# Grouped-query attention on one core: a repeating table of steps, with three of sixteen score tiles on VectorE

## The chip, the cores and the metric

The kernel runs on one core of one Trainium2 chip. The metric is device time in microseconds (us). Three timed runs of the kernel before took 431.78, 433.16 and 433.04 us; the median is 433.04 us. A profile of one execution goes with them.

## The reference

Q has 8 batches, 512 queries, 32 heads and 64 columns; K and V have 8 K heads, and four Q heads share each K head.

```python
K_expanded = np.repeat(K, heads_per_group, axis=2)
V_expanded = np.repeat(V, heads_per_group, axis=2)
...
scores = np.einsum('bhqd,bhkd->bhqk', Q, K_expanded) * scale
weights = np.exp(scores - np.max(scores, axis=-1, keepdims=True))
weights = weights / (np.sum(weights, axis=-1, keepdims=True) + 1e-10)

output = np.einsum('bhqk,bhkd->bhqd', weights, V_expanded)
```

All arrays are float32. `scale` is 1/8.

## The kernel before

The kernel takes exp of the scaled scores without subtracting a maximum, sums the rows with an extra column of ones beside V, and checks afterwards that the sums lie within bounds. If they do not, a second, slow path (`general_path`) runs; with these inputs it does not. Both kernels have it, and it plays no part here.

**Units, jobs, pairs, tiles.** A unit is two K heads of one batch, so there are 32 units. A job is one K head with its four Q heads, so a unit holds two jobs and the kernel 64. A job has two pairs of Q heads. Scores are held transposed: 128 keys on the partitions, 512 queries along them. One tile is the scores of one pair against 128 keys, that is two heads of 512 queries, 1024 columns. A pair has four such tiles, a job 8, a unit 16.

**The way of a tile.** TensorE writes it into PSUM with two matmuls of 64 contraction rows (`scores`, L209). Of the 8 tiles of a job, seven go through `s_ps` (two buffers) to ScalarE, whose exp (L227) writes float16 weights into `pt`. The eighth goes through `d_ps` (one buffer, shared with the transposes) to VectorE, which makes exp out of bits in a chain of five instructions:

- u (L238): scale and add, from PSUM to int16 in SBUF
- f (L259, in `exp_d2`): the low ten bits of u
- g (L251) and w (L255): a quadratic correction; in most jobs (`by_pool`) both run on GpSimd, in the first three and in the last on VectorE
- the join (L272, in `exp_d4`): u + w, written into `pt` as the bits of a float16

g, w and the join read and write SBUF alone, as f does. u reads PSUM.

**Weights times V.** For each pair, 32 matmuls of 65 columns (L303, `pv`) accumulate in `pv` (one buffer). VectorE then takes the reciprocal of the sums (L336) and multiplies (L340, `norm`), reading PSUM, into `o_sb`, which SyncE stores (L380).

**Transposes and loads.** Q comes in through GpSimd's DMA queue with a cast to bfloat16, a transfer for each unit (L126). TensorE transposes it (L164), VectorE copies it out of PSUM (L167). K is loaded for each batch (L103) and transposed by SyncE's DMA queue. V is loaded for each batch in four transfers (L111). `check_v` (L177, L184) multiplies each V head with itself to bound its size.

**Order.** The schedule is manual: each engine works through its own instructions in the order in which the program issues them, which is the loop over jobs at L423 to L505. In it, the parts of job j (scores and exp) alternate with those of job j-1 (`pv` and `norm`). Around VectorE's chain it reads:

```python
        if late and by_pool(last):
            exp_d4(last)
        exp_d2(j)
```

So the join of the last job comes directly ahead of f of this job, and GpSimd's g and w start only after f.

Of the kernel before, what the change touches and what calls it, by code (L numbers as in the profile page):

```python
# [36 lines left out]
WIDE = lambda j: False  # L37
# [21 lines left out]
def fast_path(ctx, tc, Q, K, V, out, flag):  # L59
# [7 lines left out]
    NPAIR = HPG // 2  # L67
    scale = 1.0 / math.sqrt(D)
    A_U = 1024.0 / math.log(2.0) * scale
    B_U = 15.0 * 1024.0 + 1024.0 * math.log2(EXP_S)  # L70
    SPB = 16

    const_pool = ctx.enter_context(tc.tile_pool(name="const", bufs=1))
    qnat_pool = ctx.enter_context(tc.tile_pool(name="qnat", bufs=4))
# [4 lines left out]
    dve_pool = ctx.enter_context(tc.tile_pool(name="dve", bufs=2))  # L79
    osb_pool = ctx.enter_context(tc.tile_pool(name="osb", bufs=3))  # L80
    inv_pool = ctx.enter_context(tc.tile_pool(name="inv", bufs=3))
# [14 lines left out]
    vt = [const_pool.tile([128, SC, KV, D + 1], BF16, name=f"v{j}") for j in range(2)]  # L96
# [11 lines left out]

    def load_v(b, lo=0, hi=KV):
        for sc in range(SC):  # L110
            nc.gpsimd.dma_start(  # L111
                out=vt[b % 2][:, sc, lo:hi, 0:D],
                in_=V[b, sc * 128:(sc + 1) * 128, lo:hi, :],
            )

    def load_v_head(b, g):
        nc.gpsimd.dma_start(
            out=vt[b % 2][:, :, g, 0:D], in_=V[b, :, g, :].rearrange("(sc p) d -> p sc d", p=128)
        )

    def load_q(u, cuts=(0, 2 * HPG)):
        b, gp = divmod(u, GP)
        h0 = gp * 2 * HPG
        qn[u] = qnat_pool.tile([128, SC, 2 * HPG, D], BF16, name="q_nat")
        for lo, hi in zip(cuts[:-1], cuts[1:]):
            nc.gpsimd.dma_start(  # L126
                out=qn[u][:, :, lo:hi, :],
                in_=Q[b, :, h0 + lo:h0 + hi, :].rearrange("(sc p) h d -> p sc h d", p=128),
            )
# [3 lines left out]

# [21 lines left out]

    def trans_q(j, bank, lo=0, hi=NPAIR):
        u, g = divmod(j, 2)
        ps = bank.bitcast(BF16).rearrange("p (i sc c) -> p i sc c", i=NPAIR, sc=SC)  # L160
        for i in range(lo, hi):
            for sc in range(SC):
                h = g * HPG + 2 * i
                nc.tensor.transpose(ps[:, i, sc, :], qn[u][:, sc, h:h + 2, :], ident)  # L164
        if u not in qt:
            qt[u] = qt_pool.tile([128, 2, NPAIR, S], BF16, name="qt")
        return lambda: nc.vector.tensor_copy(  # L167
            out=qt[u][:, g, lo:hi, :], in_=ps[:, lo:hi, :, :].rearrange("p i sc c -> p i (sc c)")
        )


    def check_v(u, bank):
        b, gp = divmod(u, GP)
        for g in range(2):
            for sc in range(SC):
                v = vt[b % 2][:, sc, 2 * gp + g, 0:D]
                nc.tensor.matmul(  # L177
                    bank[64 * g:64 * g + 64, 0:D],
                    v,
                    v,  # L180
                    start=(sc == 0),
                    stop=(sc == SC - 1),
                )
        return lambda: nc.vector.tensor_reduce(  # L184
            out=okv[:, u:u + 1], in_=bank[:, 0:D], op=ALU.max, axis=AX.X
        )

    NJOB = NU * 2  # L190
    DPAIR = NPAIR - 1

    def taken(j):
        return 3 if WIDE(j) else 2

    def act_tiles(j):
        every = [(i, kc, m) for i in range(NPAIR) for kc in range(SC) for m in range(2)]
        first = DPAIR * SC * 2
        mine = [n for n in range(len(every)) if not first <= n < first + taken(j)]
        groups = [[n for n in mine if n // 2 == h] for h in range(len(every) // 2)]  # L200
        return [[every[n] for n in group] for group in groups if group]

    jobs, osb, invs, ends = {}, {}, {}, []

    def scores(j, ps, i, kc, m):
        u, g = divmod(j, 2)
        b, gp = divmod(u, GP)
        keys = kt_first[:, gp, :, :] if b == 0 else kt[b][:, :, gp, :]
        nc.tensor.matmul(  # L209
            ps,  # L210
            keys[64 * m:64 * m + 64, g ^ m, kc * 128:(kc + 1) * 128],
            qt[u][64 * m:64 * m + 64, g, i, :],
            start=True,
            stop=True,
        )

    def open_job(j):
        pt = pt_pool.tile([128, NPAIR, SC, 2, S], FP16, name="pt")
        jobs.setdefault(j, {}).update(pt=pt, pv={})

    def act_tile(j, n):
        group = act_tiles(j)[n]
        i, kc, lo = group[0]
        ps = s_pool.tile([128, 2, S], FP32, name="s_ps")
        for _, _, m in group:
            scores(j, ps[:, m, :], i, kc, m)
        nc.scalar.activation(  # L227
            out=jobs[j]["pt"][:, i, kc, lo:, :], in_=ps[:, lo:, :], func=EXP, scale=scale
        )

    def exp_d(j, lo, hi, ps):
        st = jobs.setdefault(j, {})
        if "u" not in st:
            for name, dtype in (("u", I16), ("f", I16), ("g", BF16), ("w", BF16)):
                st[name] = dve_pool.tile([128, 3, S], dtype, name=name + "16")[:, 0:taken(j), :]
        for n in range(lo, hi):
            scores(j, ps[:, n - lo, :], DPAIR, n // 2, n % 2)
        return lambda: nc.vector.tensor_scalar(  # L238
            out=st["u"][:, lo:hi, :], in0=ps[:, 0:hi - lo, :], scalar1=A_U, scalar2=B_U,
            op0=ALU.mult, op1=ALU.add,  # L240
        )


    def by_pool(j):
        return 3 <= j < NJOB - 1

    def correction(engine, f, g, w):
        as_bits = engine is nc.gpsimd  # L250
        engine.tensor_scalar(  # L251
            out=g, in0=f, scalar1=-EXP_F1, scalar2=EXP_K * 2.0 ** (24 * as_bits),
            op0=ALU.add, op1=ALU.mult,
        )
        engine.tensor_tensor(out=w, in0=g, in1=f.bitcast(FP16) if as_bits else f, op=ALU.mult)  # L255

    def exp_d2(j):
        st = jobs[j]
# [3 lines left out]
        if by_pool(j):  # L262
            exp_d3(j, nc.gpsimd)

    def exp_d3(j, engine):
        st = jobs[j]
        correction(engine, st["f"], st["g"], st["w"])

    def exp_d4(j):
        st = jobs[j]  # L270
        n = taken(j)
        nc.vector.tensor_tensor(  # L272
            out=st["pt"][:, DPAIR, :, :, :].rearrange("p kc m q -> p (kc m) q")[:, 0:n, :].bitcast(
                U16
            ),
            in0=st["u"],
            in1=st["w"],
            op=ALU.add,
        )

    def blocks(j, i):
        if j == NJOB - 1:
            kcs = (0, 1, 2, 3) if i == 0 else (2, 0, 1, 3)
        else:
            kcs = (2, 3, 1, 0)
        return [(kc, m, qc) for kc in kcs for m in range(2) for qc in range(SC)]

    def pv(j, i, lo, hi):
        st = jobs[j]
        u, g = divmod(j, 2)  # L290
        b, gp = divmod(u, GP)
        if lo == 0:

            if j < NJOB - 1:
                t = pv_pool.tile([128, 2, S], FP32, name="pv")
            else:
                t = d_tile() if i == 0 else s_pool.tile([128, 2, S], FP32, name="s_ps")
            t = t.rearrange("p m (qc c) -> p m qc c", qc=SC)
            st["pv"][i] = t[:, :, :, 0:D + 1]
        order = blocks(j, i)  # L300
        for n in range(lo, hi):
            kc, m, qc = order[n]
            nc.tensor.matmul(  # L303
                st["pv"][i][:, m, qc, :],
                st["pt"][:, i, kc, m, qc * 128:(qc + 1) * 128],
                vt[b % 2][:, kc, 2 * gp + g, :],
                start=(n < 2 * SC and qc == 0),
                stop=(n >= len(order) - 2 * SC and qc == SC - 1),
            )
# [11 lines left out]
    def norm(j, i):  # L321
        st = jobs[j]
        u, g = divmod(j, 2)
        sums = st["pv"][i]
        if u not in osb:
            osb[u] = osb_pool.tile([128, SC, 2 * HPG, D], FP32, name="o_sb")
        p = j * NPAIR + i
        left = NJOB * NPAIR - p
        k, n = divmod(p, SPB)
        if left <= NLAST:  # L330
            inv = inv_last[:, NLAST - left]
        else:
            if k not in invs:
                invs[k] = inv_pool.tile([128, SPB, 2, SC], FP32, name="inv")
            inv = invs[k][:, n]
        nc.vector.reciprocal(out=inv, in_=sums[:, :, :, D:D + 1])  # L336
        if left == 1:
            last_check()
        h = g * HPG + 2 * i
        nc.vector.tensor_tensor(  # L340
            out=osb[u][:, :, h:h + 2, :].rearrange("p qc m d -> p m qc d"),
            in0=sums[:, :, :, 0:D],
            in1=inv[:, :, :, None].to_broadcast((128, 2, SC, D)),
# [4 lines left out]
        elif g == 1 and i == NPAIR - 1:  # L348
            store(u, 0, 2 * HPG)
        if left > NLAST and (n == SPB - 1 or left == NLAST + 1):  # L350
            cols = (n + 1) * 2 * SC
            flat = invs.pop(k).rearrange("p s m qc -> p (s m qc)")[:, 0:cols]
# [10 lines left out]

    def last_check():
# [8 lines left out]
        count = pv_pool.tile([128, 2, S], FP32, name="pv")  # L373
# [11 lines left out]

    def probe():
# [4 lines left out]
        correction(nc.gpsimd, f, g, w)  # L391
# [4 lines left out]


# [5 lines left out]
    for j in range(2):  # L403
        nc.gpsimd.memset(vt[j][:, :, :, D:D + 1], 1.0)
    load_v_head(0, 0)
# [218 lines left out]
```

## Time and profile before

| What | Value |
|---|---|
| median of the three runs | 433.04 us (431.78 to 433.16) |
| span of the profiled execution, first to last instruction | 431.5 us |
| what lies around the span, by the three times | 0.3 to 1.7 us |
| ScalarE busy | 413.5 us (96%) |
| TensorE busy | 392.3 us (91%) |
| VectorE busy | 309.3 us (72%) |
| GpSimd busy | 254.1 us (59%) |
| exp on ScalarE (L227) | 448 instructions, 412.2 us |
| steady part, 86.0 to 137.3 us | 51.3 us for four units |

The profile gives no total time for the profiled execution itself; its span is set against the three times. Busy time is the time in which at least one instruction of the engine was in work; neighbouring instructions overlap, so a mean duration times a count can be above it. TensorE's ends are modelled, so its 91% does not say that it is full. Shares over the whole span mix a start, a steady part and an end; here the steady part is long, from about 34 to 424 us.

### The profile page before, as it was taken

How to read it: one execution, taken by the hardware profiler on the slowest of the kernel's cores; microseconds unless marked ns; L12 is line 12 of the kernel's file. 1: busy time of each engine (PE TensorE's matmuls, PEld its weight loads, DVE VectorE, ACT ScalarE, POOL GpSimd, SP SyncE). 2: the span in 40 equal slices, each digit the busy share in tenths (PEclk: the TensorE clock that was granted, in tenths of full speed). 3: DMA queues.
4: the chain of work that ended last, by engine and by line, in shares of the span. 5: the costliest groups of instructions: out<-in, count | busy, mean ns of one | idle time of the engine just before them, and what ended most of it. 6: DMA issues, size and time to landing. Idle time of an engine off the chain costs nothing.

```text
span 431.5 us, 13531 instructions
## 1 busy us (share of the span) xinstructions
PE 392.3 (91%) x5945; PEld 249.6 (58%) x5945; DVE 309.3 (72%) x585; ACT 413.5 (96%) x449; POOL 254.1 (59%) x212
## 2 busy tenths in 40 slices
PE   6889999999999999999999999999999999999984
PEld 2455566556556556556556556566555655655653
DVE  2587778767777767776767876876777776777765
ACT  3889999999999999999999999999999999999993
POOL 8805464965468566595457756497546856545530
PEclk8599999999999999999999999999999999999998
DMA  9998645898649986499946979689954998622214
GB/s 101 173 167 186 171 137 146 124 182 202 154 128 195 143 201 150 119 212 125 259 78 161 191 89 287 149 115 196 204 143 136 187 156 195 151 99 99 99 72 130
DMA packets 91439, 66.97 MB, mean 155 GB/s; under 512 B 52080, under 2 KB 74608, under 8 KB 91376
## 3 DMA queue, kind: packets, MB, share of 16 engines
q0 software_dynamic: 56544, 25.17, 49.9%
q1 hardware_dynamic: 34832, 40.90, 34.9%
q8 instruction: 47, 0.77, 0.7%
q14 instruction: 16, 0.13, 0.1%
HBM read 50.33 MB, written 33.55 MB: 194 GB/s over the span
## 4 chain that ended last, share of the span: by engine, by line
ACT 65%; PE 28%; DVE 4%; issue 1%; POOL 1%; ACTq 0%; DVEq 0%; POOLq 0%
ACT pt L227 65%; PE s_ps L209 12%; PE pv L303 10%; PE d_ps L164 5%; DVE o_sb L340 1%; DVE w L255 0%; DVE pt L272 0%; POOL q_nat L126 0%; DVE qt L167 0%; DVE kt_first L146 0%; PE d_ps L143 0%; DVE g L251 0%; PE d_ps L145 0%; POOL k_nat L103 0%; ACTq L227 0%
## 5 line engine op out<-in xcount | busy, mean ns | idle before, releaser
L227 ACT ACTIVATE pt<-s_ps 128x1024 f16<-128x1024 f32 x448 | 412.2, 1115 | 9.6 <-PE s_ps L209 9.3
L303 PEld LDWEIGHTS <-pt 128*128 128x128 f16 x4096 | 142.8, 98 | 78.2 <-issue 56.1
L303 PE MATMUL pv<-v,pt 128*128 128x65 bf16 x4032 | 178.8, 195 | 3.5 <-DVE o_sb L340 2.5
L209 PE MATMUL s_ps<-qt,kt 64*128 64x512 bf16 x784 | 153.7, 382 | 23.8 <-ACT pt L227 8.6
L251 POOL TENSOR_SCALAR g<-f 128x1024 bf16<-128x1024 int16 x60 | 62.4, 1039 | 154.5 <-DVE f L259 154.5
L255 POOL TENSOR_TENSOR w<-g,f 128x1024 bf16<-128x1024 bf16 x60 | 127.5, 2125 | 5.0
L209 PEld LDWEIGHTS <-kt 64*128 64x128 bf16 x896 | 59.5, 93 | 62.6 <-issue 26.8
L340 DVE TENSOR_TENSOR o_sb<-pv,inv 128x512 f32<-128x512 f32 x125 | 86.4, 691 | 4.3
L336 DVE RECIPROCAL inv<-pv 128x8 f32<-128x8 f32 x125 | 25.7, 206 | 85.4 <-PE pv L303 85.4
L238 DVE TENSOR_SCALAR u<-d_ps 128x1024 int16<-128x1024 f32 x64 | 77.7, 1214 | 0.7 <-PE d_ps L209 0.7
L167 DVE COPY qt<-d_ps 128x1024 bf16<-128x1024 bf16 (+1 forms) x65 | 44.3, 683 | 20.1 <-PE d_ps L177 12.1
L272 DVE TENSOR_TENSOR pt<-u,w 128x1024 uint16<-128x1024 int16 x64 | 43.6, 681 | 0.2
L164 PE MATMUL d_ps<-ident,q_nat 128*128 128x128 bf16 x512 | 40.7, 224 | 0.9 <-DVE kt_first L146 0.9
L164 PEld LDWEIGHTS <-q_nat 128*128 128x128 bf16 x512 | 29.5, 99 | 16.0 <-issue 14.9
L259 DVE TENSOR_SCALAR f<-u 128x1024 int16<-128x1024 int16 x64 | 29.6, 463 | 0.1
L126 POOL DMA_DIRECT2D q_nat<-in_Q_dram x34 | 27.3, 803 | 1.5 <-DMA q_nat<-in_Q_dram 1.2
L111 POOL DMA_DIRECT2D v<-in_V_dram x32 | 28.2, 890 | 0.0
L209 PE MATMUL s_ps<-qt,kt_first 64*128 64x512 bf16 x112 | 24.4, 431 | 2.6 <-ACT pt L227 1.1
L209 PE MATMUL d_ps<-qt,kt 64*128 64x512 bf16 x112 | 21.4, 376 | 0.0
L209 PEld LDWEIGHTS <-kt_first 64*128 64x128 bf16 x128 | 7.6, 96 | 10.8 <-issue 6.5
L177 PE MATMUL d_ps<-v 128*64 128x64 bf16 x256 | 10.4, 201 | 0.0
L177 PEld LDWEIGHTS <-v 128*64 128x64 bf16 x256 | 6.9, 110 | 3.3 <-issue 0.2
(46 smaller groups left out, 52.4 us busy)
## 6 DMA issues: line engine op xcount, KB each, us to landing
out_dram<-o_sb SPq DMA_DIRECT2D x31, 1024.0 KB, 5.9
q_nat<-in_Q_dram POOLq DMA_DIRECT2D x31, 512.0 KB, 7.5
k_nat<-in_K_dram POOLq DMA_DIRECT2D x7, 512.0 KB, 7.7
v<-in_V_dram POOLq DMA_DIRECT2D x28, 128.0 KB, 8.8
kt<-kt SPq DMA_DIRECT2D x14, 256.0 KB, 4.2
out_dram<-o_sb SPq DMA_DIRECT2D x4, 256.0 KB, 2.4
kt<-k_nat SPq DMA_TRANSPOSE x28, 8.7
v<-in_V_dram POOLq DMA_DIRECT2D x4, 96.0 KB, 8.2
```

Source lines behind the costliest of these rows:

```text
L111: nc.gpsimd.dma_start(out=vt[b % 2][:, sc, lo:hi, 0:D], in_=V[b, sc * 128:(sc + 1) * 128, lo:hi, :],)
L164: nc.tensor.transpose(ps[:, i, sc, :], qn[u][:, sc, h:h + 2, :], ident)
L167: return lambda: nc.vector.tensor_copy(out=qt[u][:, g, lo:hi, :], in_=ps[:, lo:hi, :, :].rearrange("p i sc c -> p i (sc c)"))
L209: nc.tensor.matmul(ps, keys[64 * m:64 * m + 64, g ^ m, kc * 128:(kc + 1) * 128], qt[u][64 * m:64 * m + 64, g, i, :], start=True, stop=True,)
L227: nc.scalar.activation(out=jobs[j]["pt"][:, i, kc, lo:, :], in_=ps[:, lo:, :], func=EXP, scale=scale)
L238: return lambda: nc.vector.tensor_scalar(out=st["u"][:, lo:hi, :], in0=ps[:, 0:hi - lo, :], scalar1=A_U, scalar2=B_U, op0=ALU.mult, op1=AL ...
L251: engine.tensor_scalar(out=g, in0=f, scalar1=-EXP_F1, scalar2=EXP_K * 2.0 ** (24 * as_bits), op0=ALU.add, op1=ALU.mult,)
L255: engine.tensor_tensor(out=w, in0=g, in1=f.bitcast(FP16) if as_bits else f, op=ALU.mult)
L259: nc.vector.tensor_single_scalar(out=st["f"], in_=st["u"], scalar=1023, op=ALU.bitwise_and)
L272: nc.vector.tensor_tensor(out=st["pt"][:, DPAIR, :, :, :].rearrange("p kc m q -> p (kc m) q")[:, 0:n, :].bitcast(U16), in0=st["u"], in1=st ...
L303: nc.tensor.matmul(st["pv"][i][:, m, qc, :], st["pt"][:, i, kc, m, qc * 128:(qc + 1) * 128], vt[b % 2][:, kc, 2 * gp + g, :], start=(n < 2 ...
L340: nc.vector.tensor_tensor(out=osb[u][:, :, h:h + 2, :].rearrange("p qc m d -> p m qc d"), in0=sums[:, :, :, 0:D], in1=inv[:, :, :, None].t ...
```

## The change

The loop over jobs and its helpers are replaced by a table of tokens, `STEPS`, which is gone through once for each unit (a step). A token names a part of the work and an index; `@1` means that it is done for the unit before, and `@-1` for the one after, so that neighbouring units overlap. The tokens: S fills a score tile for ScalarE and A takes its exp; D fills one for VectorE; U, F, G, W and P are u, f, g, w and the join; V is a part of weights times V; R and N are the reciprocal and the multiplication; T and C are the transposes and their copy; H reads the V check; Q stands for the loads.

- VectorE takes the last tile of pairs 1, 2 and 3 of each unit (of pairs 2 and 3 in unit 0): 3 of 16 where it had 2. ScalarE takes 13, where it had 14. All units but the first and the last have g and w on GpSimd.
- Q is loaded for two units with one transfer, three buffers instead of four smaller ones.
- V holds, for two K heads together, one column of ones, 128 columns of V, one column of ones. It is loaded in four transfers for a batch, half of them in each of two steps. The check of V takes four matmuls of 128 columns for a unit instead of eight of 64.
- `dve_pool` has four buffers for each name instead of two; the limits on sums are looked at for 32 pairs at once instead of 16.

The single `d_ps` and `pv` buffers and the two `s_ps` buffers stay.

```diff
+DVE_KCS = ((), (3,), (3,), (3,))
+STEPS = (
+    "A0 V1.2-4@1 G2@1 S1 H0@1 P1@1 V1.4-6@1 A1 V1.6-8@1 S2 R1@1 D0a W2@1 N1@1 A2 S3 U0 "
+    "V2.0-2b@1 A3 V2.2-4@1 S4 V2.4-6@1 A4 F0 V2.6-8@1 S5 R2@1 G0 T0a N2@1 A5 S6 C0 V3.0-2b@1 "
+    "W0 V3.2-3@1 A6 P2@1 S7 D1a V3.3-5@1 A7 U1 S8 V3.5-8@1 A8 S9 R3@1 D2a N3@1 A9 S10 F1 "
+    "V0.0-1b U2 V0.1-3 G1 A10 V0.3-4 S11 V0.4-7 P0 A11 V0.7-8 W1 S12 Q0 R0 T1a N0 A12 S0@-1 "
+    "F2 V1.0-1b C1 V1.1-2 "
+).split()
...
-    qnat_pool = ctx.enter_context(tc.tile_pool(name="qnat", bufs=4))
+    qnat_pool = ctx.enter_context(tc.tile_pool(name="qnat", bufs=3))
...
-    vt = [const_pool.tile([128, SC, KV, D + 1], BF16, name=f"v{j}") for j in range(2)]
+    VW = 2 * D + 2
+    vt = [const_pool.tile([128, SC, GP, VW], BF16, name=f"v{j}") for j in range(2)]
...
+    def exp_fill(u, k, ps):
+        scores(u, *ON_DVE[k], ps)
+        st = chain[u, k] = {"ps": ps}
...
+    def slope(engine, f, g):
+        engine.tensor_scalar(
+            out=g, in0=f, scalar1=-EXP_F1,
+            scalar2=EXP_K * 2.0 ** (24 * (engine is nc.gpsimd)),
+            op0=ALU.add, op1=ALU.mult,
+        )
+
+    def bend(engine, f, g, w):
+        f = f.bitcast(FP16) if engine is nc.gpsimd else f
+        engine.tensor_tensor(out=w, in0=g, in1=f, op=ALU.mult)
+
+    def exp_join(u, k):
+        p, kc = ON_DVE[k]
+        st = chain.pop((u, k))
         nc.vector.tensor_tensor(
+            out=pt_of(u, p)[:, kc, :, :].bitcast(U16), in0=st["u"], in1=st["w"], op=ALU.add
+        )
...
+    def loads(u):
+        b, gp = divmod(u, GP)
...
+        if u >= 2 and u % 2 == 0 and u + 4 < NU:
+            load_q(u // 2 + 2)
+        if b + 1 < B:
+            if gp == 1:
+                load_k(b + 1)
+            if gp in (1, 2):
+                for sc in (0, 1) if gp == 1 else (2, 3):
+                    load_v_rows(b + 1, sc)
...
+    for period in range(-1, NU + 3):
+        for entry in STEPS:
+            tok, _, late = entry.partition("@")
+            u = period - int(late or 0)
+            if 0 <= u < NU:
+                step(tok, u)
```

## The prediction

> **What bounds the kernel now.** I read the busy shares first, then the chain that ended last, then three steady windows, then the costliest groups.
>
> ```profile
> PE 392.3 (91%) x5945; PEld 249.6 (58%) x5945; DVE 309.3 (72%) x585; ACT 413.5 (96%) x449; POOL 254.1 (59%) x212
> ...
> ACT 65%; PE 28%; DVE 4%; issue 1%; POOL 1%; ACTq 0%; DVEq 0%; POOLq 0%
> ...
> L227 ACT ACTIVATE pt<-s_ps 128x1024 f16<-128x1024 f32 x448 | 412.2, 1115 | 9.6 <-PE s_ps L209 9.3
> ```
>
> ScalarE has 96% of the span and carries the chain; it idles 9.6 us in all, nearly all before 34 us. The windows give the steady part (busy us of PE, PEld, DVE, ACT, POOL, each with its count):
>
> ```profile
> 86.00:137.30 51.30, 47.82 (x738) 30.76 (x736) 37.57 (x72) 51.30 (x57) 32.55 (x26) 1.00 0.92 166
> ```
>
> ScalarE is never idle there, at a granted TensorE clock of 1.00. 51.3 us is one batch, four units, so a unit costs 12.83 us. It holds 14 exp tiles, which mostly start 0.904 us apart (14 x 0.904 = 12.66; twice in a unit TensorE's transposes cost some 0.08 more).
>
> **What a step can cost at best.** With 13 tiles ScalarE needs 13 x 0.904 = 11.75 us. The other engines, by differences of starts in the timeline near 200 us:
>
> TensorE: a pair of score matmuls holds it about 0.32 us, a V matmul 0.031, eight transposes 0.55. A step is 16 x 0.32 + 128 x 0.031 + 1.1 + 0.2 (V check) = 10.4 us: it fits.
>
> VectorE: reciprocal 0.24, multiplication 0.61, u 1.12, join 0.60, f 0.36, copy of Q 0.61, V check 0.2. A step is 3 x 2.08 + 4 x 0.85 + 2 x 0.61 + 0.2 = 11.1 us: it fits, with 0.6 us to spare.
>
> GpSimd: g to w 1.12 us, w to the next 2.06, so 3.18 for a chain, 9.5 for three. A batch's loads are one of K (0.75), four of V (0.87; its pieces halve in number and double in width, so 0.75, as K's, to 0.87; I take the upper end), two of Q (0.82; twice the bytes in the same number of pieces; no row has such, 0.75 to 0.87): 5.9 us, 1.5 a step. In all 11.0 us: it fits.
>
> So by the sums ScalarE would stay the bound. But these sums hold only if the engines don't hold each other, and the trace has rows that say they do.
>
> **The row against it.** The timeline of VectorE, then of GpSimd, at one load of V:
>
> ```profile
> 85.36 0.68 DVE L272 TENSOR_TENSOR pt<-u,w 128x1024 uint16<-128x1024 int16 x1
> 85.96 0.83 DVE L259 TENSOR_SCALAR f<-u 128x1024 int16<-128x1024 int16 x1
> ...
> 83.01 3.56 POOL L111 DMA_DIRECT2D v<-in_V_dram  x4
> 86.89 1.04 POOL L251 TENSOR_SCALAR g<-f 128x1024 bf16<-128x1024 int16 x1 [0.32 <-DVE f L259]
> ```
>
> GpSimd issues V's loads until 86.57. f begins at 85.96 and takes 0.83 us instead of 0.42: it ends 0.22 us after GpSimd does. Of the 64 f's, the eight that begin beside such an issue take 487 to 841 ns, all others 416 to 427. The same over the whole run:
>
> ```profile
> L259 DVE TENSOR_SCALAR f<-u x64: 416/418/841, 11.4 to 419.4; 128x1024 int16<-128x1024 int16 x64
> ...
> L340 DVE TENSOR_TENSOR o_sb<-pv,inv x125: 690/691/692, 19.8 to 420.5; 128x512 f32<-128x512 f32 x125
> ...
> L272 DVE TENSOR_TENSOR pt<-u,w x64: 679/680/693, 15.0 to 423.4; 128x1024 uint16<-128x1024 int16 x64
> ...
> L255 POOL TENSOR_TENSOR w<-g,f x60: 2120/2125/2133, 35.9 to 414.6; 128x1024 bf16<-128x1024 bf16 x60
> ```
>
> The multiplication (L340), which reads PSUM, runs beside GpSimd's g and w in most jobs and never changes. f, from SBUF to SBUF, is made to wait. The join has not been tried: of 64, 51 run with GpSimd idle, 12 beside a DMA issue (680 ns, not held) and one beside a probe; none beside a g or w. The kernel before keeps them apart, since the join waits for w, f comes directly behind the join, and g waits for f. In GpSimd's 45% of free time they cost nothing. The change takes that cover away.
>
> **What meets what.** I lay one step out with A k starting at 0.904 k and the durations above. u of chain 0 stands behind the multiplication of pair 1, 2.1 to 3.3; F0 follows, 3.3 to 3.7. G0 runs 3.7 to 4.8, W0 4.9 to 7.0. P2 of the unit before stands behind C0, at 5.6: inside W0. F1 comes at 8.4, GpSimd being free; G1 8.8 to 9.9, W1 9.9 to 12.0. P0 stands behind U2, at 9.9, and F2 at 11.3: both inside W1. G2 and W2 follow in the next step (0.3 to 3.5), P1 at 0.7 inside G2, F0 at 3.3 inside W2. So five of six f's and joins start beside a g or w. Held until the end of it, they would wait 0.2 (F0), 1.4 (P2), about 2 (P0, with F2 then behind it) and 0.6 (P1): 4 us against VectorE's 0.6 us to spare.
>
> Behind a held VectorE instruction, in order, stand the reciprocal and multiplication. The single `pv` buffer waits for these, so TensorE stops at the next V, and the score tiles behind it in TensorE's queue come late to ScalarE. That is the new wait I expect. `d_ps` makes a second one: U1 late makes D2 late.
>
> **The price.** The layout shifts once things are held, so I price it by GpSimd's time, where held work adds up: while an f or join has the path, GpSimd's arithmetic stands, and the other way round. Lower bound: none of it held, 11.0, and ScalarE's 11.75 decides. Upper: all six held in full, 11.0 + 3 x (0.42 + 0.68) = 14.3 us. The V-load row shows that about 0.20 of an instruction passes beside the other's end; off each of six: 13.1 us. Between 13.1 and 14.3 I take 13.8: above the middle (13.7), since GpSimd also waits for an f that is itself late, and little above it, since F1 and joins beside a load pass free. For the join the ends are 0 and 0.68; I take it as held, because it is nearer to f (SBUF only) than to the multiplication (PSUM).
>
> The Trainium skill, page "SBUF — State Buffer", section "Who interferes with whom", says that a VectorE instruction with two SBUF inputs contends with a GpSimd instruction that reads SBUF, and that the loser waits for the whole instruction; this trace shows the like for f beside DMA issues, and no run here shows the join beside g or w. By that rule in full, my estimate from it is the upper 14.3 us and about 482 us.
>
> **The rest.** Fewer V and Q transfers, the V check (8 matmuls to 4) and the check of sums lie on engines that don't decide: 0, covered by ScalarE's tiles or, now, by VectorE's waits. The loads stand behind W1 and ahead of G2 in GpSimd's queue (in the sum above); SyncE's transposes of K are issued two units ahead of their use, so moving them costs 0 while their 8.7 us to landing fit two steps. Start: the same first loads, 14 ScalarE tiles in unit 0, no GpSimd arithmetic there: 0, bound -2 to +3 (before lost some 4 us to gaps there). End: before, the last multiplication (426.91) ends 2.9 us after the last exp. After, behind the last exp stand F2's inline chain (0.36 + 0.37 + 0.6 + 0.6), R1 and N1 (0.9), pair 2's V (32 x 0.031 + 0.2), R2, N2, R3, check, N3 (2.1): 6.1 us, so +3. The last unit has the chains on VectorE: 11.1 + 3 x 1.0 = 14.1, the same as the others here.
>
> Sum, on the profiled execution: 431.5 + 31 x (13.8 - 12.83) + 3 = 464.6 us; 1.5 around the span (433.04 - 431.5): **466 us**. Against the median that is +7.6%. It breaks even at a step of 12.73 us.
>
> **Rivals.**
>
> A, the forecast: 0.60. Its own range is 13.1 to 14.6 us a step, 444 to 491 us.
>
> B, faster: neither g nor w holds f or the join, since only the writing of descriptors does. For it: every long f has a DMA issue beside it; the join never moves beside one. Against: f has no row beside g or w, so its freedom isn't shown. ScalarE then bounds at 11.75; in two steps of four GpSimd has 9.5 + 2.5 = 12.0. Mean 11.9: 431.5 - 28.8 + 3 + 1.5 = 407 us. It decides as soon as held time is under 1.6 us a step. 0.20.
>
> C: f is held and the join not (its 12 rows at 680). Step 11.0 + 3 x 0.42 = 12.3: 420 us. 0.10.
>
> D: nothing is held, but VectorE at 11.1 of 11.75 doesn't keep step, as every R waits for V and every U for D: about 2 us a step of idle in front of R (before: 85.4 us in 64 jobs, 2.7 a unit). Step 13.1: 444 us. 0.07.
>
> The rest, 0.03, is a mixture that ends at about 433. That the share doesn't move is no rival: the built order has 13 tiles and three chains a step.
>
> **How the numbers follow.** Slower: A + D = 0.67; faster: B + C = 0.30; same: 0.03 (0.3% is about what a measurement of this kernel tells from no change). The range reaches down to B's time, leaving half of B, and up to near A's end: 407 to 488. A alone: 444 to 491.
>
> **What will show it.** Right: joins and f's with long durations (over 1 us where w is in work), g and w unchanged or longer, ScalarE idle before tiles with TensorE waiting for the multiplication, about 13.8 us a step. Wrong: joins at 680 ns beside w (B, C), ScalarE over 95% busy (B); f alone long (C); VectorE idle before R and nothing stretched (D).

## The result: 18% slower, and the profile after

The changed kernel takes 511.72 us (510.0 to 512.12, four runs) against 432.83 us (431.78 to 433.16); the ratio is 1.1814, interval 1.179 to 1.1839. The profiled execution spans 510.3 us and took 511.91.

The page of the changed kernel, busy shares, chain, and the groups that answer to those shown before:

```profile
PE 393.3 (77%) x5817; PEld 237.4 (47%) x5817; DVE 468.5 (92%) x672; ACT 401.0 (79%) x418; POOL 349.3 (68%) x257
...
DVE 63%; PE 22%; DMA 6%; issue 3%; POOL 2%; ACT 2%; SPq 1%; DVEq 0%; ACTq 0%; POOLq 0%
...
L229 ACT ACTIVATE pt<-s_ps 128x1024 f16<-128x1024 f32 x417 | 399.7, 1031 | 94.1 <-PE s_ps L215 73.1
...
L260 POOL TENSOR_TENSOR w<-g,f 128x1024 bf16<-128x1024 bf16 x90 | 207.7, 2308 | 7.5
...
L265 DVE TENSOR_TENSOR pt<-u,w 128x1024 uint16<-128x1024 int16 x95 | 117.7, 1239 | 0.3
...
L247 DVE TENSOR_SCALAR f<-u 128x1024 int16<-128x1024 int16 x95 | 90.6, 954 | 1.1
L322 DVE TENSOR_TENSOR o_sb<-pv,inv 128x512 f32<-128x512 f32 x125 | 86.4, 691 | 4.3
```

ScalarE has its 31 tiles less (417 for 448) and now idles 94.1 us. The chain that ended last has moved from ScalarE to VectorE. The join's mean has gone from 0.68 to 1.24 us and f's from 0.46 to 0.95, while the multiplication, which reads PSUM, still takes 0.691. The idle time in front of the join and f is next to nothing: an instruction that is held is not shown as a wait, but as a long instruction.

By the source view (shortest, median, longest ns) the two are far from uniform:

```profile
L265 DVE TENSOR_TENSOR pt<-u,w x95: 672/692/2535, 23.6 to 499.9; 128x1024 uint16<-128x1024 int16 x95
...
L247 DVE TENSOR_SCALAR f<-u x95: 415/427/2154, 21.9 to 498.2; 128x1024 int16<-128x1024 int16 x95
```

The timeline of a step of the changed kernel, VectorE, then GpSimd, TensorE and ScalarE (start, duration, and in brackets the idle time before):

```profile
201.52 2.31 DVE L265 TENSOR_TENSOR pt<-u,w 128x1024 uint16<-128x1024 int16 x1
...
207.19 0.68 DVE L265 TENSOR_TENSOR pt<-u,w 128x1024 uint16<-128x1024 int16 x1
...
208.63 1.50 DVE L247 TENSOR_SCALAR f<-u 128x1024 int16<-128x1024 int16 x1
...
210.86 1.40 DVE L265 TENSOR_TENSOR pt<-u,w 128x1024 uint16<-128x1024 int16 x1
...
212.42 0.69 DVE L322 TENSOR_TENSOR o_sb<-pv,inv 128x512 f32<-128x512 f32 x1
...
201.16 2.13 POOL L260 TENSOR_TENSOR w<-g,f 128x1024 bf16<-128x1024 bf16 x1
...
207.36 2.50 POOL L260 TENSOR_TENSOR w<-g,f 128x1024 bf16<-128x1024 bf16 x1
...
210.69 1.04 POOL L252 TENSOR_SCALAR g<-f 128x1024 bf16<-128x1024 int16 x1
...
213.16 0.67 PE L282 MATMUL pv<-v,pt 128*128 128x65 bf16 x16 [1.57 <-DVE o_sb L322]
...
214.20 4.70 ACT L229 ACTIVATE pt<-s_ps 128x1024 f16<-128x1024 f32 x5 [1.47 <-PE s_ps L215]
```

The join at 201.52 begins inside the w of 201.16 and ends at 203.83, 0.54 us after that w (203.29). The f at 208.63 ends 0.27 after the w of 207.36. The join at 210.86 ends 0.53 after the g of 210.69. This holds in every case beside a w: 28 joins begin there, take 0.91 to 2.54 us, and end 0.54 to 0.55 us after it; 44 f's begin there and end 0.28 to 0.29 us after it, or 0.32 for the one that meets only its tail. Of the 47 joins that begin beside a g, 17 are held likewise (0.95 to 1.41 us); the other 30 begin in its last 0.09 us and take 0.68. It goes the other way too: the w of 207.36 meets the join of 207.19 and takes 2.50 us instead of 2.13. Three rows show the damage: the held join delays the multiplication (212.42), TensorE stops 1.57 us for it at the next V (213.16), and ScalarE stops 1.47 us for its tile (214.20).

**Where the 78.8 us of span went**, by the starts of ScalarE's first tile of each unit:

| Part of the span | before | after | difference |
|---|---|---|---|
| to the first exp | 8.44 | 8.45 | 0.0 |
| unit 0 | 15.5 | 18.2 | 2.7 |
| units 1 to 30 | 387.0 (12.90 each) | 454.6 (15.15 each) | 67.6 |
| unit 31 to the end | 20.5 | 29.0 | 8.5 |

In units 8 to 27 a step takes 15.19 us. VectorE is busy 14.70 of them: 1.85 by which joins and 1.79 by which f's are longer than 0.680 and 0.418 us, and 11.06 that are left, the 11.1 of the work at the durations of before. GpSimd is busy 11.29, ScalarE has 11.75 to do. The granted clock of TensorE is 0.97 from 200 to 300 us, beside 1.00 in the kernel before; what share this has was not tried, but VectorE idles only 0.49 us of the step.

### The profile page after: what moved, and what is told of

Read it like the earlier page. It is cut to its first block, busy times and chain, and to the rows that moved or that the text cites. A ratio compares the mean times of both kernels' runs of the same rounds, so it can differ in the third digit from the quotient of the medians.

```text
span 510.3 us, 13368 instructions
## 1 busy us (share of the span) xinstructions
PE 393.3 (77%) x5817; PEld 237.4 (47%) x5817; DVE 468.5 (92%) x672; ACT 401.0 (79%) x418; POOL 349.3 (68%) x257
## 4 chain that ended last, share of the span: by engine, by line
DVE 63%; PE 22%; DMA 6%; issue 3%; POOL 2%; ACT 2%; SPq 1%; DVEq 0%; ACTq 0%; POOLq 0%
DVE pt L265 16%; DVE o_sb L322 13%; PE pv L282 12%; DVE f L247 12%; DVE u L241 10%; PE s_ps L215 7%; DVE qt L179 6%; DVE inv L311 3%; DMA kt<-k_nat 2%; DMA k_nat<-in_K_dram 2%; ACT pt L229 2%; DMA q_nat<-in_Q_dram 2%; PE d_ps L176 2%; DVE okv L188 1%; SPq L164 1%
## 5 line engine op out<-in xcount | busy, mean ns | idle before, releaser
L229 ACT ACTIVATE pt<-s_ps 128x1024 f16<-128x1024 f32 x417 | 399.7, 1031 | 94.1 <-PE s_ps L215 73.1
L260 POOL TENSOR_TENSOR w<-g,f 128x1024 bf16<-128x1024 bf16 x90 | 207.7, 2308 | 7.5
L252 POOL TENSOR_SCALAR g<-f 128x1024 bf16<-128x1024 int16 x90 | 94.1, 1045 | 127.7 <-DVE f L247 126.1
L265 DVE TENSOR_TENSOR pt<-u,w 128x1024 uint16<-128x1024 int16 x95 | 117.7, 1239 | 0.3
L241 DVE TENSOR_SCALAR u<-d_ps 128x1024 int16<-128x1024 f32 x95 | 115.3, 1214 | 2.2 <-PE d_ps L215 2.2
L247 DVE TENSOR_SCALAR f<-u 128x1024 int16<-128x1024 int16 x95 | 90.6, 954 | 1.1
L215 PEld LDWEIGHTS <-kt 64*128 64x128 bf16 x896 | 39.9, 93 | 56.8 <-issue 33.4
L215 PE MATMUL d_ps<-qt,kt 64*128 64x512 bf16 x168 | 33.1, 385 | 16.1 <-DVE u L241 9.7
L135 POOL DMA_DIRECT2D q_nat<-in_Q_dram x19 | 15.1, 798 | 0.0
L187 PE MATMUL d_ps<-v 128*128 128x128 bf16 x128 | 12.8, 224 | 0.0
L215 PEld LDWEIGHTS <-kt_first 64*128 64x128 bf16 x128 | 6.2, 95 | 14.2 <-issue 10.5
```

What stands on the lines that cost most here:

```text
L215: nc.tensor.matmul(ps[:, m, :], keys[64 * m:64 * m + 64, g ^ m, kc * 128:(kc + 1) * 128], qt[u][64 * m:64 * m + 64, g, i, :], start=True, ...
L229: nc.scalar.activation(out=pt_of(u, p)[:, kc, :, :], in_=filled.pop((u, p, kc)), func=EXP, scale=scale)
L241: nc.vector.tensor_scalar(out=st["u"], in0=st["ps"], scalar1=A_U, scalar2=B_U, op0=ALU.mult, op1=ALU.add)
L247: nc.vector.tensor_single_scalar(out=st["f"], in_=st["u"], scalar=1023, op=ALU.bitwise_and)
L252: engine.tensor_scalar(out=g, in0=f, scalar1=-EXP_F1, scalar2=EXP_K * 2.0 ** (24 * (engine is nc.gpsimd)), op0=ALU.add, op1=ALU.mult,)
L260: engine.tensor_tensor(out=w, in0=g, in1=f, op=ALU.mult)
```

## The experiments

Two theories stood against each other. Theory 1: f and the join are held while GpSimd's g and w are in work. Theory 2: VectorE's queue and the single `d_ps` and `pv` buffers can't keep the table's step, whatever GpSimd does. All edits but one are made to the changed kernel. Where no spread is given, the kernel was timed once.

### GpSimd's arithmetic taken out

```diff
-                if what == "G":
-                    slope(nc.gpsimd, st["f"], st["g"])
-                elif what == "W":
-                    bend(nc.gpsimd, st["f"], st["g"], st["w"])
-                elif what == "P":
+                if what == "P":
...
-            out=pt_of(u, p)[:, kc, :, :].bitcast(U16), in0=st["u"], in1=st["w"], op=ALU.add
+            out=pt_of(u, p)[:, kc, :, :].bitcast(U16), in0=st["u"],
+            in1=st["w"] if u == 0 or u == NU - 1 else st["f"].bitcast(BF16), op=ALU.add
```

> The changed kernel without g and w on GpSimd: the join adds f's bits, read as bfloat16 (next to nothing), in place of w, so the correction of the exp is left out; every VectorE instruction, its order and all transfers stay. Theory 1 (f and joins are held while GpSimd's g and w run): joins 0.68 us, f 0.42 us except beside a DMA issue, VectorE back to 11.1 us of work a step, ScalarE the bound at 11.75 to 12.1 us; with the changed kernel's longer start and end some 415 to 425 us. Theory 2 (VectorE's queue and the single d_ps and pv buffers can't keep the table's step, whatever GpSimd does): joins wait less for w, but the step stays near 14 to 15 us, 475 to 510 us.

Measured: 418.26 us, beside 432.19 for the kernel before. A step takes 11.97 us. The join and f by source, and the window from 200 to 300 us (busy us of PE, PEld, DVE, ACT, POOL):

```profile
L265 DVE TENSOR_TENSOR pt<-u,f x90: 674/680/683, 38.6 to 394.5; 128x1024 uint16<-128x1024 int16 x90
...
L247 DVE TENSOR_SCALAR f<-u x95: 415/417/584, 21.6 to 404.5; 128x1024 int16<-128x1024 int16 x95
...
200.00:300.00 100.00, 95.27 (x1503) 60.66 (x1499) 94.86 (x170) 99.81 (x110) 10.37 (x14) 1.00 0.85 179
```

None of these 90 joins is above 0.683 us, and ScalarE is full again. VectorE has the same list of instructions in the same order as in the changed kernel, so the list alone costs 12 us a step and not 15: theory 2 falls as the cause of the loss. The run also takes away the join's wait for w; the long durations above show that this wait was not the cost (0.3 us of idle time in front of 95 joins).

### GpSimd writing only

```diff
-                    slope(nc.gpsimd, st["f"], st["g"])
+                    nc.gpsimd.tensor_copy(out=st["g"][0:1, 0, 0:1], in_=st["f"][0:1, 0, 0:1])
+                    nc.gpsimd.memset(st["g"], 0.0)
...
-                    bend(nc.gpsimd, st["f"], st["g"], st["w"])
+                    nc.gpsimd.memset(st["w"], 0.0)
+                    nc.gpsimd.memset(st["w"], 0.0)
```

> The changed kernel with g replaced on GpSimd by a copy of one element and a memset of g, and w by two memsets of w to zero (the correction is left out): GpSimd is about as long busy, behind the same f, but its long instructions only write SBUF. If what holds a join is GpSimd's reading: joins 0.68 us beside the memsets, f (if it needs the writing side too) still held, VectorE saves the joins' 1.85 us of holding a step, 13.2 to 13.6 us, about 455 to 470 us. If any GpSimd instruction in work holds both: joins up to 1.9 us, no change beyond the memsets' own length, 490 to 515 us. Theory 2: 490 to 515 us as well, but with joins and f's at their short durations.

Measured: 431.07 us beside 432.19; 12.18 us a step. GpSimd is busy 73% of the span, more than the 68% of the changed kernel, 10.2 us a step. By source:

```profile
L265 DVE TENSOR_TENSOR pt<-u,w x95: 674/680/693, 22.9 to 418.9; 128x1024 uint16<-128x1024 int16 x95
...
L247 DVE TENSOR_SCALAR f<-u x95: 415/427/1212, 21.3 to 417.2; 128x1024 int16<-128x1024 int16 x95
```

The join is not held by instructions that only write SBUF: the 75 that begin beside a memset take at most 0.683 us. f is held: the 50 that begin beside one end 0.28 to 0.33 us after it. So GpSimd's being busy does not hold the join; g and w differ from the memsets in that they read SBUF. The time came out below what was expected: a memset is short (0.95 us), and an f waits only for the one in work, 0.23 us in the mean. The Trainium skill, page "SBUF — State Buffer", section "Who interferes with whom", states just this pair: two SBUF inputs contend with a GpSimd instruction that reads SBUF, not with one that only writes it, and two-port instructions contend with both. This case agrees, with 0.68 us as the longest join beside a memset and 2.54 beside w. That f is such a two-port instruction, no run here shows directly.

### The joins moved

```diff
-    "A0 V1.2-4@1 G2@1 S1 H0@1 P1@1 V1.4-6@1 A1 V1.6-8@1 S2 R1@1 D0a W2@1 N1@1 A2 S3 U0 "
-    "V2.0-2b@1 A3 V2.2-4@1 S4 V2.4-6@1 A4 F0 V2.6-8@1 S5 R2@1 G0 T0a N2@1 A5 S6 C0 V3.0-2b@1 "
-    "W0 V3.2-3@1 A6 P2@1 S7 D1a V3.3-5@1 A7 U1 S8 V3.5-8@1 A8 S9 R3@1 D2a N3@1 A9 S10 F1 "
-    "V0.0-1b U2 V0.1-3 G1 A10 V0.3-4 S11 V0.4-7 P0 A11 V0.7-8 W1 S12 Q0 R0 T1a N0 A12 S0@-1 "
-    "F2 V1.0-1b C1 V1.1-2 "
+    "A0 V1.2-4@1 G2@1 S1 H0@1 V1.4-6@1 A1 V1.6-8@1 S2 R1@1 D0a W2@1 N1@1 A2 S3 U0 "
+    "V2.0-2b@1 A3 V2.2-4@1 S4 V2.4-6@1 A4 P2@1 F0 V2.6-8@1 S5 R2@1 G0 T0a N2@1 A5 S6 C0 V3.0-2b@1 "
+    "W0 V3.2-3@1 A6 S7 D1a V3.3-5@1 A7 U1 S8 V3.5-8@1 A8 S9 R3@1 D2a N3@1 A9 S10 P0 F1 "
+    "V0.0-1b U2 V0.1-3 G1 A10 V0.3-4 S11 V0.4-7 A11 V0.7-8 W1 S12 Q0 R0 T1a N0 A12 S0@-1 "
+    "P1 F2 V1.0-1b C1 V1.1-2 "
```

> The changed kernel with each join moved directly ahead of an f that comes before the next g (P2 ahead of F0, P0 ahead of F1, P1 ahead of F2), the order that the kernel before has; all work stays. Theory 1: joins and f's meet no g or w and take 0.68 and 0.42 us; the join waits for w instead, and GpSimd's loop w, join, f, g, w becomes the limit: 3 x (3.2 + 1.1) = 12.9 us and the loads on top, 13.3 to 14.3 us a step, 455 to 485 us. Theory 2: the same work in nearly the same order, within 2% of the changed kernel, 500 to 520 us.

Measured: 499.42 us; 14.68 a step. The groups of VectorE:

```profile
L265 DVE TENSOR_TENSOR pt<-u,w 128x1024 uint16<-128x1024 int16 x95 | 65.4, 688 | 75.3 <-POOL w L260 75.0
...
L247 DVE TENSOR_SCALAR f<-u 128x1024 int16<-128x1024 int16 x95 | 39.8, 419 | 0.1
```

The mechanism is as theory 1 has it: nothing is held any more, 0.688 and 0.419 us. The time is a miss for both theories' figures, though near theory 2's. What the holding cost has come back as 75 us in which VectorE stands still for w: join, f, g and w follow each other in a loop of 4.4 us (joins at 250.04 and 254.45), and VectorE's queue, in order, waits with it. Three loops are 13.2 us, already over the 12.83 of before, and one of the three is longer still. So this order doesn't repair the third tile: the two engines no longer meet, but take turns. Other orders were not tried.

### The correction on VectorE

```diff
     def by_pool(u):
-        return 1 <= u < NU - 1
+        return False
```

> The changed kernel with g and w on VectorE in all units, so GpSimd issues loads alone. VectorE gets three times g (0.37 us) and w (0.60), 2.9 us more work a step. Theory 1: 11.1 + 2.9 = 14.0 us with nothing held but f or g beside a DMA issue, so 14.0 to 14.4 us a step against 15.15: faster than the changed kernel in spite of the added work, 475 to 490 us. Theory 2: the queue only gets fuller, 15.15 + 2.9 = 18 us a step, about 600 us.

Measured: 552.65 us, 16.51 a step: slower than the changed kernel, a miss for theory 1's 475 to 490 us and below theory 2's 600. Nothing is held here (joins 0.69 us), but VectorE is busy 14.9 us a step and idles 1.6. The added 2.9 us of the estimate came to 3.5 (14.9 against 11.4 in the run without GpSimd's arithmetic): instructions that need each other's results start 0.45 us (f to g), 0.47 (g to w) and 0.79 (w to join) apart in the chain at 252.76, where the estimate had 0.36, 0.37 and 0.60. Standing together, the chain also holds up the reciprocals behind it: TensorE's weight loads for the V matmuls wait 99.8 us in all for multiplications, and ScalarE idles 135 us. Theory 2 has this share: once VectorE is the bound, its order and waits count in full. It does not explain the changed kernel, whose list ran at 12 us a step above.

### GpSimd's instructions cut in four

```diff
+                quarters = [(m, slice(q, q + S // 2)) for m in range(2) for q in (0, S // 2)]
...
-                    slope(nc.gpsimd, st["f"], st["g"])
+                    for h in quarters:
+                        slope(nc.gpsimd, st["f"][:, h[0], h[1]], st["g"][:, h[0], h[1]])
...
-                    bend(nc.gpsimd, st["f"], st["g"], st["w"])
+                    for h in quarters:
+                        bend(nc.gpsimd, *(st[n][:, h[0], h[1]] for n in "fgw"))
```

> The changed kernel with each g and each w cut into four GpSimd instructions of 256 columns; the results and all else are the same. If a join or f waits until the GpSimd instruction in work ends (theory 1): at most about 0.6 us instead of 2.1, joins below 1.0 us and f's below 0.7 in the mean, VectorE's step from 14.7 to 12.5 to 13.2 us of work; GpSimd pays for 24 starts instead of 6 and is itself stopped at each meeting, so 13 to 14 us a step, 445 to 475 us. If GpSimd's next instruction gets ahead of the waiting VectorE instruction: joins stay at 1.2 us or more and the time at 510 us or above.

Measured: 558.92 us, above every figure expected for theory 1. Groups of VectorE and GpSimd:

```profile
L265 DVE TENSOR_TENSOR pt<-u,w 128x1024 uint16<-128x1024 int16 x95 | 66.4, 699 | 104.0 <-POOL w L260 103.3
...
L247 DVE TENSOR_SCALAR f<-u 128x1024 int16<-128x1024 int16 x95 | 52.0, 548 | 1.1
...
L260 POOL TENSOR_TENSOR w<-g,f 128x256 bf16<-128x256 bf16 x360 | 240.1, 696 | 7.2
L252 POOL TENSOR_SCALAR g<-f 128x256 bf16<-128x256 int16 x360 | 186.5, 518 | 50.8 <-DVE f L247 22.6
```

Holding does shrink with the length of the instruction, as theory 1 said: joins 0.70 us, f's 0.55. But a quarter costs far more than a quarter of a whole (in the mean, meetings included, w 0.70 us against 2.13 / 4 = 0.53 and g 0.52 against 1.04 / 4 = 0.26; the medians are 0.67 and 0.40), GpSimd needs 4.7 us a chain, and now VectorE waits 103 us for w. The starts were underpriced, so the time tells nothing between the theories, and part of the joins' short durations may come from their waiting for w first.

### Two tiles in the new table

```diff
-DVE_KCS = ((), (3,), (3,), (3,))
+DVE_KCS = ((), (3,), (), (3,))
```

with the tokens of one chain taken out of the table, one S and A more, and each join directly ahead of an f.

> The changed kernel with VectorE's share undone: two of sixteen tiles (pairs 1 and 3), ScalarE 14, the table thinned out to match, each join directly ahead of an f as in the kernel before; the table itself, Q for two units, V with ones on both sides and the overlap stay. If the loss comes from the third tile alone (VectorE held, theory 1): ScalarE bounds again at 14 x 0.904 = 12.66 to 12.8 us a step, with the changed kernel's start (+3) and end (+5 to +8) 435 to 443 us. If the table or the loads cost something of their own in the steady part: over 13.2 us a step, over 455 us.

Measured: 442.55 us (441.0 to 443.03) against 432.54; ratio 1.0217, interval 1.0184 to 1.0249. Units 8 to 27 take 12.83 us each, to the hundredth what the kernel before takes, with ScalarE at 100.00 of 100 us. So the table, the loads of Q and the layout of V cost and bring nothing in the steady part; there the whole loss goes with the third tile and with the places of the joins, which this run puts back together. What is left over, 9 us of span, lies in unit 0 (18.7 us against 15.5, with 15 ScalarE tiles against 14), from unit 31 to the end (26.4 against 20.5), and with 0.6 ahead of the first exp.

### Half a tile more in the kernel before

```diff
-WIDE = lambda j: False
+WIDE = lambda j: j % 2 == 0 and j > 8
```

> The kernel before with one half tile more on VectorE in every second job from job 10 on (27 jobs, its own switch), so 2.5 of 16 on average there; join directly ahead of f, so neither meets g or w. ScalarE saves about 0.4 us in each of 27 jobs, 11 us: 422 us if the chain fits. Against it: in a wide job GpSimd needs 1.5 x 3.2 = 4.8 us, with join and f (1.5 us, one after the other with it) 6.3 of the job's 6.2 us, and loads come on top: the join then waits for w and VectorE's queue with it, 430 to 445 us. Theory 1 leans to the second.

Measured: 432.72 us (431.67 to 433.33) against 432.54; ratio 1.0003, interval 0.9988 to 1.0017. No change, and not for the reason expected. By form, ScalarE:

```profile
L227 ACT ACTIVATE pt<-s_ps 128x1024 f16<-128x1024 f32 x421 | 392.8, 1053 | 14.9 <-PE s_ps L209 14.6
L227 ACT ACTIVATE pt<-s_ps 128x512 f16<-128x512 f32 x27 | 18.8, 697 | 0.0
```

The half tile takes 0.70 us, but the tile after it mostly starts 0.91 us after it, as behind a whole one: it waits for TensorE. Between 200 and 300 us ScalarE is busy 98.13 instead of 100. TensorE behind the score matmul of a half tile, whose exp starts at 208.35:

```profile
208.02 0.62 PE L164 MATMUL d_ps<-ident,q_nat 128*128 128x128 bf16 x8
208.57 0.33 PE L177 MATMUL d_ps<-v 128*64 128x64 bf16 x8
208.83 0.39 PE L209 MATMUL s_ps<-qt,kt 64*128 64x512 bf16 x2
```

The transposes of Q and the V check stand ahead of the next tile's score matmuls in TensorE's queue, and these follow without a gap; so it is in 26 of the 27 cases. What half a tile saves on ScalarE is lost to this order of TensorE's work, not to joins that wait for w (0.3 us of idle time in front of 64 joins). No run that does the whole computation beat the kernel before.

## Why the prediction was wrong in size and right in kind

**Right.** The forecast was A: VectorE and GpSimd hold each other, ScalarE starves, slower. The named signs are all there: joins over 1 us beside w, w longer, ScalarE idle with TensorE waiting for the multiplication. The row it was read from, an f of 0.83 us beside a load of V, gave the tail right as well: f ends 0.22 us after GpSimd there, 0.28 here. The guess that the join is like f, not like the multiplication, held; rivals B and C fall with it, and D with the step of 11.97 us.

**The meetings.** The layout said F0 0.2, P2 1.4, P0 about 2 with F2 behind it, and P1 0.6 us, 4.2 in all. Measured, averaged over the run: F0 0.74 (in some units nothing, in others up to 1.74), P2 1.5, P0 0, F2 0.96, P1 0.23. That is 3.5, and 3.64 in units 8 to 27. So the sum is near, but partly by luck, for the places have shifted: P0, which the layout had at the start of W1, begins 0.17 us ahead of it in every unit and is not held (W1 is, 2.50 us), while F0 and F2 are held longer than the layout had them.

**The step that failed** is "I price it by GpSimd's time, where held work adds up", the term of 13.8 us a step. It measured 15.19. GpSimd is not the engine that fills up: it is busy 11.29 us a step and waits 126 us in the run for f's. What fills up is VectorE: 11.06 + 1.85 + 1.79 = 14.70, and 0.49 idle. The prediction had both numbers on the page, 11.1 us of work and 4.2 of holding, and added them to the wrong queue. On VectorE's queue it would have read 15.3 us a step and 431.5 + 31 x (15.3 - 12.83) + 3 + 1.5 = 513 us, against 511.72. That this comes so near is luck in part: the holding of 4.2 us is 0.6 too much, no idle time is in it, and the start and the end are 8 us too low (below). The upper bound, 14.3 us for "all six held in full", was no bound, since it counted f's and joins at their own length while a held one stands for up to the length of GpSimd's instruction. So the range ended at 488, too low.

**Start and end.** Unit 0 was put at 0, bound -2 to +3, and measured +2.7. In it TensorE waits 2.96 us for Q of unit 1, which the table transposes in the step of unit 0. The end was put at +3 and measured +8.5, of which most is behind the last exp: from there to the end of the last multiplication the sum had 6.1 us, and it took 10.5 (496.0 to 506.46). The chains are on VectorE in the last unit, and TensorE works in bursts between waits of 2.4 and 3.3 us for multiplications. TensorE in the timeline of the changed kernel:

```profile
497.00 1.14 PE L282 MATMUL pv<-v,pt 128*128 128x65 bf16 x32 [2.38 <-DVE o_sb L322]
501.48 1.94 PE L282 MATMUL pv<-v,pt 128*128 128x65 bf16 x32 [3.34 <-DVE o_sb L322]
```

The last 5 us of work in the windows (columns as above, the last but two being the granted clock):

```profile
502.00:507.00 5.00, 3.36 (x59) 3.10 (x56) 2.15 (x7) 0.00 (x0) 0.00 (x0) 0.50 0.37 105
```

The granted clock is 0.50 in this window, 0.82 in the one from 494 to 502, and the 32 matmuls that begin at 501.48 take 1.94 us, where the 32 at 497.00 took 1.14. These parts are read from the trace; which share of the 8.5 us each has was not tried.

**Readings that were off without bearing on the time.** GpSimd was idle for 41% of the span before, not 45%. The kernel before lost 1.8 us to gaps of ScalarE in unit 0, and 3.3 in the whole run behind the first exp (9.6 less the 6.3 ahead of it), not some 4. The 14.6 us at the top of A's own range has no working; the bound worked out was 14.3.

## What to carry to other kernels

Work that is free on two engines' own sums need not be free on both at once: look in the trace of before for the few instructions that run longer beside another engine's work, and price each meeting by what is left of the other's instruction. Add the held time to the queue of the engine that is held and has the least to spare, and take the largest of the engines' sums; a bound made on the other engine is none. An engine with 28% idle time by share had 0.6 us to spare in the step that the change asked for.

## What the runs showed of the hardware

- The join, a VectorE instruction with two SBUF inputs, that starts beside GpSimd's w, which reads SBUF, ends 0.54 to 0.55 us after it (28 of 28, of 0.91 to 2.54 us, against 0.68 alone); an f, 0.28 us after it (43 of 44, against a whole duration of 0.42 alone). GpSimd's w, starting while a join is in work, takes 2.43 to 2.51 us instead of 2.12 (47 of 47).
- Memsets on GpSimd don't hold the join (75 began beside one, 0.683 us at most), but hold f (up to 1.21).
- The same columns in four pieces kept GpSimd busy 2.67 us a chain instead of 2.13 for w (240.1 / 90) and 2.07 (186.5 / 90) instead of 1.05 for g, meetings included.
- A half tile on ScalarE took 0.70 us, two thirds of a whole one's 1.05.
